# One activation table at a time in the recurrent branch: copies, grouped gelus, and the softplus ahead of its loop

## The chip, the cores and the metric

The kernel runs on one core of a Trainium2 chip. The metric is the device time of one execution in microseconds (us). The engines are named as in the profile: PE (TensorE, matmuls) with PEld (its weight loads), DVE (VectorE), ACT (ScalarE), POOL (GpSimd) and SP (SyncE, whose queue issues nearly all DMAs).

## The reference

One layer of a hybrid network on 512 tokens of width 1024, with 16 meta tokens in front (528 positions). One large projection gives the inputs of two branches, a recurrent one and a retention one; a convolutional feed-forward layer follows. What the change touches is the recurrent branch:

```python
z = xn @ w_in[l]
u_rnn, u_gate, q, k, v, g_ret, ga, gb = jnp.split(z, IN_SPLITS, axis=-1)
xr = causal_dwconv(u_rnn, rnn_conv_w[l], rnn_conv_b[l])        # 4 taps, 1280 channels
hr = rg_lru(xr, ...)
o_a = hr * jax.nn.gelu(u_gate)

def rg_lru(x, w_a, b_a, w_x, b_x, lam):                        # 10 blocks of 128 channels
    r = sigmoid(x @ w_a + b_a);  i = sigmoid(x @ w_x + b_x)    # block by block
    log_a = -8 * r * softplus(-lam)
    a = exp(log_a)
    b = sqrt(-expm1(2 * log_a)) * (i * x)
    # h[t] = a[t] * h[t-1] + b[t]
```

## The kernel before

Channels lie on the 128 partitions and positions along the free axis. Every float32 matrix is held as a float16 high part and a float16 low part, and a product is three matmuls (high x high, high x low, low x high: `SPLIT`). A `split` is one ACT instruction (the high part, line 94) and one DVE instruction (the low part, line 95). Weights come in units of up to 1 MB through three staging buffers `raw`. A unit of 8 x 256 rows and columns becomes two tiles `wt`; it serves two channel blocks. The splits of the units to come are queued as steps. `tick()` issues the next step if no more than `ahead` tiles are split in advance, and `get(u)` issues all that unit u still needs.

The recurrent branch works on 10 blocks of 128 channels (`NR`), n = 0 to 9, in two loops.

The convolution loop (line 689) takes for each n the projection of block n (`conv_product`; blocks 0 to 2 had half of it earlier), the two gate products of block n - 3 (`rnn_gates`, with two sigmoids on ACT and one product on DVE), the four taps of block n (`conv_taps`: an identity on ACT, three multiply-adds on DVE, which free the PSUM buffer), and the split of the convolved block (`conv_split`). For n < 6 the projection runs with `turns`: for each of the eight slices of the depth it does both halves of the positions with the high weights and the high input, then both with the high weights and the low input, then both with the low weights. Block n uses the weights of unit n // 2. At n = 2 a `tick()` issues the split of the first tile of unit 2, at n = 3 that of the second, both of which block 4 is the first to use.

Behind this loop stand the 23 small DVE instructions and the two of ACT that compute the softplus of lambda for all channels (lines 711 to 727), and then the gate loop (line 732). For each n it projects block n of u_gate and takes the gelu straight out of PSUM (line 737). For n < 3 it also does the gates of blocks 7, 8 and 9. A table `SPREAD` places the rest, five blocks at a time: tangents `rnn_tanh` (n = 2 and 4), exponentials `rnn_decay` with two DVE products each (n = 3 and 5), roots `rnn_root` (n = 7 and 9), and the first five scans `rnn_scan` (a DVE product and a DVE scan, n = 7).

Up to line 754 the order of PE, ACT and DVE is written out by hand (`manual_schedule`): each of these engines issues its instructions in the order of the program. Instructions that stand behind it may be slipped in between by the planner, and from there on the planner orders the work by its own costs and by program order as the priority. What follows is the rotary stage: for each of four heads `rotary` projects the queries and then the keys (two PSUM buffers each), DVE multiplies each by the cosine and the sine (`t`, lines 773 to 775), which frees the buffers, and ACT and DVE split the result (`qk`). `between(i)` is called behind each of these eight steps: for i < 5 it does scan 5 + i, and it multiplies the finished blocks with their gelus and splits them (`branch_a`, `oa`). There are four PSUM buffers (`acc`) from n = 2 of the convolution loop on, used in turn by all of these products.

Each function of ACT belongs to a table that must be loaded; the instruction that loads it shows in the profile as ACT_TABLE_LOAD on the line of the function that needs it.

Of the kernel before, what the change touches and what calls it, by code (L numbers as in the profile page):

```python
# [8 lines left out]
F32 = mybir.dt.float32  # L9
F16 = mybir.dt.float16  # L10
AF = mybir.ActivationFunctionType
ORDERED = {mybir.EngineType.PE, mybir.EngineType.Activation, mybir.EngineType.DVE}
ALU = mybir.AluOpType

P = 128
# [6 lines left out]
NR = DR // P  # L22
# [4 lines left out]
TQ = T - T0  # L27
# [5 lines left out]
SW = 2.0 ** 8  # L33
S_XN = 4.0
# [19 lines left out]
def hybrid_block_kernel(ctx, tc, x, meta, norm_mix_g, w_in, conv_w, conv_b, rg_a_w, rg_a_b,  # L54
                        rg_x_w, rg_x_b, lam, w_brnn, w_bret, w_out, norm_ffn_g, w_up,
                        fconv_w, fconv_b, w_down, norm_final_g, rope_t, decay_t, out):
    nc = tc.nc
    const = ctx.enter_context(tc.tile_pool(name="const", bufs=1))
# [17 lines left out]
    def acc(name):  # L76
        return psum["acc"].tile([P, 2, 512], F32, name=name, tag="acc")
# [9 lines left out]
    def piece(shape, dtype, name):  # L87
        return pieces.tile(shape, dtype, name=name, tag="s")

    def wtile(name):  # L90
        return work.tile([P, T], F32, name=name, tag="w")
# [101 lines left out]
    def unit_load(cuts=1):  # L193

        nk, ncol, parts, fast = units[len(loaded)]
        raw = wraw.tile([P, 2048], F32, name="raw")
        n = nk * ncol
        rv = raw[:, :n].rearrange("p (k c) -> p k c", k=nk)
        for k0, c0, ap in parts:
            load(rv[:, k0:k0 + ap.shape[1], c0:c0 + ap.shape[2]], ap)  # L200
        loaded.append(len(loaded))
        if fast:
            return fast_steps(rv, nk // 2, ncol // 2)
        hk = nk // 2
        hn = hk * ncol
        tiles = []

        def step(i, c):
            def run():
                if c == 0:  # L210
                    tiles.append(wsp.tile([P, 2, 1024], F16, name="wt"))
                sl = slice(c * hn // cuts, (c + 1) * hn // cuts)
                split(tiles[i][:, 0, sl], tiles[i][:, 1, sl], raw[:, i * hn:(i + 1) * hn][:, sl], SW)
            return run

        wviews.append(lambda a, k, c0, m: tiles[k // hk][:, a, k % hk * ncol + c0:k % hk * ncol + c0 + m])
        return [step(i, c) for i in range(2) for c in range(cuts)]
# [74 lines left out]
    ahead = [6]  # L292
    current = [0]

    def unit_tiles(u):
        return 4 if units[u][3] else 2

    def emit_step():
        u, run = steps[done[0]]
        while len(loaded) < min(u + 3, len(units)):  # L300
            queue(unit_load())
        run()
        done[0] += 1

    def queue(new):
        steps.extend((len(loaded) - 1, run) for run in new)
# [9 lines left out]
    def tick(n=1, late=True):  # L316


        for _ in range(n):
            if done[0] == len(steps):  # L320
                if len(loaded) == len(units):
                    return
                queue(unit_load())
            u = steps[done[0]][0]
            if sum(unit_tiles(i) for i in range(current[0], u + 1)) > ahead[0]:
                return
            if gating[0] and not late and hasattr(steps[done[0]][1], "late"):
                return
            emit_step()
# [10 lines left out]
    vt1 = const.tile([P, P], F32, name="vt1")  # L340
# [72 lines left out]
    def x_of(hi, lo):  # L413
        tv = (hi, lo)
        return lambda a, k, c0, n: tv[a][:, k, c0:c0 + n]
# [7 lines left out]
    def run_of(ps, halves, j=0, n=None):  # L423
        c0 = 512 - halves[0][1] + j
        n = n or halves[0][1] + halves[1][1]
        return ps.rearrange("p a b -> p (a b)")[:, c0:c0 + n]

    def project(ps, w, col, src, halves, nk, turns=False):

        both = [0, 1]  # L430
        for hfs in [both] if turns else [[0], [1]]:
            for k, (aw, ax), hf in [(k, s, hf) for k in range(nk) for s in SPLIT for hf in hfs]:
                    c0, n = halves[hf]
                    nc.tensor.matmul(half_of(ps, halves, hf), w(aw, k, col, P), src(ax, k, c0, n),  # L434
                                     start=k == 0 and (aw, ax) == (0, 0), stop=k == nk - 1 and aw == 1)
# [6 lines left out]
    HQ = [(XF + T0, 256), (XF + T0 + 256, 258)]  # L442
# [167 lines left out]
    half_r, half_t, half_x, gate_g = {}, {}, {}, {}  # L610

    def part(hv, n):
        if n not in hv:
            hv[n] = piece([P, T], F32, "rnn")
        return hv[n]
# [27 lines left out]
    def conv_taps(n, ps):  # L643
        xv = part(half_x, n)
        nc.scalar.activation(xv, run_of(ps, HR, 3, T), AF.Identity, scale=cwr[:, 30 + n:31 + n], bias=b_conv[:, n:n + 1])
        for j in (2, 1, 0):
            nc.vector.scalar_tensor_tensor(xv, run_of(ps, HR, j, T), cwr[:, 10 * j + n:10 * j + n + 1], xv,
                                           op0=ALU.mult, op1=ALU.add)
# [6 lines left out]
    def rnn_gates(n):  # L655
        xs = xr_split.pop(n)
        xr = part(half_x, n)
        gi = wtile("gi")
        for nm, bias, dst in (("a", b_a, part(half_r, n)), ("x", b_x, gi)):
            ps = acc("ps")  # L660
            wt = gw[nm][0][n // 4]
            project(ps, lambda a, k, c0, m: wt[:, a, n % 4 * P:n % 4 * P + P], 0, x_of(xs[:, 0], xs[:, 1]), HG, 1)
            nc.scalar.activation(dst, run_of(ps, HG), AF.Sigmoid,
                                 scale=1.0 / (SW * S_XR), bias=bias[:, n:n + 1])
        nc.vector.tensor_mul(xr, xr, gi)

    def rnn_tanh(n):
        nc.scalar.activation(part(half_t, n), part(half_r, n), AF.Tanh, scale=cpos[:, n:n + 1])
# [11 lines left out]
    def rnn_scan(n):  # L680
        r, t, xr = part(half_r, n), part(half_t, n), part(half_x, n)
        nc.vector.tensor_mul(t, t, xr)
        nc.vector.tensor_tensor_scan(xr, r, t, 0.0, op0=ALU.mult, op1=ALU.add)

    LAG = 3
    load_gates("a")
    load_gates("x")
    queue(unit_load())
    for n in range(NR):
        ps = conv_product(n)  # L690
        if n == 0:
            split_gates("a")
        if n >= LAG:
            tick(2 if n in (4, 6, 8) else 1)
            rnn_gates(n - LAG)
        conv_taps(n, ps)
        if n == 0:
            conv_split(0)
        if n == 1:
            split_gates("x")  # L700
        if n == 2:
            tick()
            conv_split(1)
            psum_layout(acc=4)
        if n >= 2:
            conv_split(n)


    lv = vt1[:, 70:80]
    sp = const.tile([P, 8, NR], F32, name="sp")  # L710
    nc.vector.tensor_scalar(sp[:, 0], lv, -1.0, 0.0, op0=ALU.mult, op1=ALU.max)
    nc.scalar.activation(sp[:, 1], lv, AF.Abs)
    nc.scalar.activation(sp[:, 2], sp[:, 1], AF.Exp, scale=-1.0)
    nc.vector.tensor_scalar_add(sp[:, 3], sp[:, 2], 2.0)
    nc.vector.reciprocal(sp[:, 4], sp[:, 3])
    nc.vector.tensor_mul(sp[:, 4], sp[:, 4], sp[:, 2])
    nc.vector.tensor_mul(sp[:, 5], sp[:, 4], sp[:, 4])
    nc.vector.memset(sp[:, 6], 1.0 / 15.0)
    for m in (13, 11, 9, 7, 5, 3, 1):
        nc.vector.tensor_mul(sp[:, 6], sp[:, 6], sp[:, 5])  # L720
        nc.vector.tensor_scalar_add(sp[:, 6], sp[:, 6], 1.0 / m)
    nc.vector.tensor_mul(sp[:, 6], sp[:, 6], sp[:, 4])
    nc.vector.scalar_tensor_tensor(sp[:, 7], sp[:, 6], 2.0, sp[:, 0], op0=ALU.mult, op1=ALU.add)
    cneg = const.tile([P, NR], F32, name="cneg")
    cpos = const.tile([P, NR], F32, name="cpos")
    nc.vector.tensor_scalar_mul(cneg, sp[:, 7], -8.0)
    nc.vector.tensor_scalar_mul(cpos, sp[:, 7], 8.0)


    ahead[0] = 6  # L730
    SPREAD = ((rnn_tanh, 2, 0), (rnn_decay, 3, 0), (rnn_tanh, 4, 5), (rnn_decay, 5, 5), (rnn_root, 7, 0), (rnn_scan, 7, 0), (rnn_root, 9, 5))
    for n in range(NR):
        ps = acc("ps")
        u, col = u_ug[n // 2], (n % 2) * P
        project(ps, get(u), col, xf, HQ, KD)
        tick()
        nc.scalar.activation(part(gate_g, n)[:, :TQ], run_of(ps, HQ),
                             AF.Gelu_apprx_tanh, scale=1.0 / (SW * S_XN))
        if n < LAG:
            rnn_gates(NR - LAG + n)  # L740
        for f, n0, m0 in SPREAD:
            if n == n0:
                for i in range(m0, m0 + 5):
                    f(i)

    oa = {}

# [30 lines left out]
            split(dst[m][:, 0, :n], dst[m][:, 1, :n], turned[m][:, :n], s)  # L778

    def between(i):  # L780
        if i < 5:
            rnn_scan(5 + i)
        for n in ((i,), (5, 6), (7, 8), (9,))[max(0, i - 4)]:
            branch_a(n)

# [442 lines left out]
    for i in range(2):  # L1228
# [5 lines left out]
        ps = branch(u_ba, oa_of, NR)  # L1234
# [311 lines left out]
    for j in range(12):  # L1546
# [21 lines left out]
        else:  # L1568
# [4 lines left out]
            for m in range(2):  # L1573
                f = 2 * j + m
# [210 lines left out]
```

## Time and profile before

| | us |
|---|---|
| median of 3 runs | 1058.48 (1058.31 to 1058.50) |
| the profiled execution | 1058.55, span 1056.8 |
| PE busy | 1038.8 (98%) |
| DVE busy | 872.0 (83%) |
| ACT busy | 594.3 (56%) |
| mean granted clock of PE | 0.999 |

The span runs from the first to the last instruction. A row of the timeline has the start, the length, the engine, the line, the operation, output<-input, the shape and the count; in brackets stands the idle time of the engine before it and what ended it. Rows of the groups have the count, then busy time and the mean in ns, then idle time. Matmuls are pipelined, so neighbouring rows of PE overlap.

### The profile page before, as it was taken

The page shows a single profiled execution, that of the slowest core. Times are in us where ns is not written, and L with a number is a line of the kernel's source. Part 1 is how long each engine was busy: PE and PEld are TensorE (multiplying, and loading weights), DVE is VectorE, ACT ScalarE, POOL GpSimd, SP SyncE. Part 2 cuts the span into 40 slices and gives each one's busy share as a digit, 9 for nine tenths or more (in the row PEclk, how much of TensorE's full clock was granted, in tenths as well). Part 3 has the DMA queues.
Part 4 walks back from the last instruction along what each step waited for, and adds up shares of the span by engine and source line. Part 5 has one row for each costly group of instructions (what it writes and reads, how often), then busy time and mean ns, then how long its engine had stood idle before and what let it go on. Part 6 is the DMA issues. An engine that isn't in the chain of part 4 may idle for free.

```text
span 1056.8 us, 21446 instructions
## 1 busy us (share of the span) xinstructions
PE 1038.8 (98%) x9187; PEld 866.2 (82%) x9187; DVE 872.0 (83%) x1327; ACT 594.3 (56%) x942; POOL 6.9 (1%) x20
## 2 busy tenths in 40 slices
PE   8999999999999999999999999999999999999997
PEld 6888888875588888888888886588888888888884
DVE  6885799989669999997797785479989898988965
ACT  7558973444356758666454453375555555454432
POOL 2000000000000000000000000000000000000000
PEclk9999999999999999999999999999999999999999
DMA  9241253331013132334333355032433324114312
GB/s 295 94 132 58 81 180 120 123 120 41 1 41 113 49 106 74 102 111 154 102 115 120 111 209 180 1 120 81 160 102 99 120 81 144 58 61 145 96 41 80
DMA packets 109311, 111.52 MB, mean 106 GB/s; under 512 B 5674, under 2 KB 101136, under 8 KB 109216
## 3 DMA queue, kind: packets, MB, share of 16 engines
q1 hardware_dynamic: 108640, 109.74, 32.5%
q8 instruction: 72, 1.18, 0.5%
q10 hardware_dynamic: 288, 0.27, 0.1%
q0 software_dynamic: 288, 0.14, 0.1%
q14 instruction: 23, 0.19, 0.1%
HBM read 108.04 MB, written 2.10 MB: 104 GB/s over the span
## 4 chain that ended last, share of the span: by engine, by line
PE 74%; DVE 15%; ACT 8%; issue 2%; DMA 0%; ACTq 0%; DVEq 0%
PE ps L434 27%; PE P L1603 10%; PE pa L886 9%; DVE wt L95 4%; PE pe L886 4%; PE ps L1320 4%; PE pm L434 3%; PE ps L448 3%; PE pb L886 2%; PE ps L950 2%; PE pa L1490 2%; ACT wt L94 2%; PE ps L1040 2%; PE pa L974 1%; DVE raw L262 1%
## 5 line engine op out<-in xcount | busy, mean ns | idle before, releaser
L434 PEld LDWEIGHTS <-wt 128*128 128x128 f16 x3840 | 372.8, 97 | 53.4 <-issue 1.3
L95 DVE SCALAR_TENSOR_TENSOR wt<-raw,wt 128x1024 f16<-128x1024 f32 (+2 forms) x286 | 310.4, 1102 | 54.0 <-ACT wt L94 52.9
L94 ACT ACTIVATE wt<-raw 128x1024 f16<-128x1024 f32 (+2 forms) x286 | 267.8, 958 | 117.8 <-PE P L1603 23.1
L886 PEld LDWEIGHTS <-wt 128*128 128x128 f16 x2016 | 195.3, 97 | 32.4 <-issue 5.7
L434 PE MATMUL ps<-x2h,wt 128*128 128x258 f16 (+1 forms) x1184 | 196.2, 273 | 0.0
L434 PE MATMUL ps<-xh,wt 128*128 128x258 f16 (+4 forms) x1056 | 177.5, 275 | 1.6 <-DVE t L773 1.6
L434 PE MATMUL ps<-x2l,wt 128*128 128x256 f16 (+1 forms) x592 | 161.0, 272 | 0.0
L434 PE MATMUL ps<-xl,wt 128*128 128x256 f16 (+4 forms) x528 | 140.8, 274 | 0.0
L1603 PE MATMUL P<-wt,act 128*128 128x256 f16 x792 | 88.3, 273 | 0.0
L1603 PEld LDWEIGHTS <-act 128*128 128x128 f16 x792 | 77.4, 98 | 9.0
L886 PE MATMUL pa<-xs,wt 128*128 128x258 f16 x576 | 71.3, 273 | 1.9 <-ACT kept L892 1.5
L1468 DVE SCALAR_TENSOR_TENSOR cv<-ps,vt,cv 128x512 f32<-128x512 f32 x80 | 59.5, 747 | 9.1 <-ACT cv L1466 8.5
L434 PE MATMUL pm<-oa,wt 128*128 128x256 f16 (+1 forms) x480 | 54.1, 273 | 0.0
L262 DVE TENSOR_TENSOR raw<-raw 128x1024 f32<-128x1024 f32 x43 | 52.5, 1220 | 0.7
L886 PE MATMUL pa<-ob,wt 128*128 128x257 f16 x384 | 45.7, 274 | 0.6 <-ACT last L892 0.5
L1320 PE MATMUL ps<-wt,mx 128*128 128x512 f16 x192 | 44.3, 379 | 0.0
L950 PE MATMUL ps<-wt,xh 128*128 128x512 f16 x128 | 38.3, 379 | 0.7 <-ACT qk L94 0.5
L1466 ACT ACTIVATE cv<-ps,vt,vt 128x512 f32<-128x512 f32 x40 | 30.5, 766 | 11.9 <-PE ps L434 11.9
L1490 PEld LDWEIGHTS <-wt 128*128 128x128 f16 x336 | 32.6, 97 | 4.4
L1320 PEld LDWEIGHTS <-mx 128*128 128x128 f16 x192 | 17.6, 98 | 18.5
L94 ACT ACTIVATE qk<-t 128x514 f16<-128x514 f32 (+1 forms) x16 | 10.2, 638 | 39.6 <-DVE t L775 39.6
L448 PEld LDWEIGHTS <-wt 128*128 128x128 f16 x288 | 27.9, 97 | 5.0 <-issue 0.5
(327 smaller groups left out, 1504.5 us busy)
## 6 DMA issues: line engine op xcount, KB each, us to landing
raw<-in_w_in SPq DMA_DIRECT2D x36, 1024.0 KB, 5.1
raw<-in_w_up SPq DMA_DIRECT2D x24, 1024.0 KB, 5.2
raw<-in_w_down SPq DMA_DIRECT2D x48, 256.0 KB, 3.7
raw<-in_w_branch_ret SPq DMA_DIRECT2D x16, 512.0 KB, 4.9
raw<-in_w_in SPq DMA_DIRECT2D x12, 512.0 KB, 4.8
raw<-in_w_branch_rnn SPq DMA_DIRECT2D x8, 640.0 KB, 4.7
raw<-in_w_out SPq DMA_DIRECT2D x4, 1024.0 KB, 5.1
xin<-in_x SPq DMA_DIRECT2D x4, 512.0 KB, 5.8
```

What stands on the lines that cost most here:

```text
L94: a = nc.scalar.activation(hi, src, AF.Copy, scale=s)
L95: b = nc.vector.scalar_tensor_tensor(lo, src, s, hi, op0=ALU.mult, op1=ALU.subtract)
L262: nc.vector.tensor_tensor(pair, pair, rv[:, :, right].rearrange("p (h k) c -> p h k c", h=2), op=ALU.add)
L434: nc.tensor.matmul(half_of(ps, halves, hf), w(aw, k, col, P), src(ax, k, c0, n), start=k == 0 and (aw, ax) == (0, 0), stop=k == nk - 1 and ...
L448: mm = nc.tensor.matmul(half_of(ps, halves, hf), w(aw, k, col, P), src(ax, k, c0, n), start=k == 0 and (aw, ax) == (0, 0), stop=k == KD - ...
L886: nc.tensor.matmul(ps[:, :n], ws[k // 4](wf, aw, k % 4), src(xf_, ax, k), start=first and k == 0 and (aw, ax) == (0, 0), stop=k == last_k ...
L950: nc.tensor.matmul(pb, xf(ax, k, XF + j0, nb), w(aw, k % 4, 0, 512), start=i == 0, stop=i == 23)
L1320: nc.tensor.matmul(ps[:, n], mx[k][:, a, c0:c0 + P], wo[k // 2](aw, k % 2, n * 512, 512), start=k == 0 and (a, aw) == (0, 0), stop=k == ks ...
L1466: nc.scalar.activation(vv_, taps[2], AF.Identity, scale=vt2[:, 96 + ch:97 + ch], bias=bias)
L1468: nc.vector.scalar_tensor_tensor(vv_, taps[j], vt2[:, 48 * j + ch:48 * j + ch + 1], vv_, op0=ALU.mult, op1=ALU.add)
L1490: nc.tensor.matmul(ps[:, :258], w(wf, aw, k), x2_form(xf_, ax, k), start=first and k == 0 and (aw, ax) == (0, 0), stop=k == 3 and aw == 1, ...
L1603: nc.tensor.matmul(pd[:, 256 * tt:256 * tt + 256], t[:, ax, c0 + tt * P:c0 + tt * P + P], w(wf, aw, i), start=q % 6 == 0 and tt == 0 and i ...
```

## The change

The softplus becomes a function that is called at n = 2 of the convolution loop, ahead of that turn's `tick()`; its series is written with fewer instructions (16 on DVE). The tangent of block n - 3 is taken in turn n of that loop, those of blocks 7, 8 and 9 in the gate loop. In the gate loop the projections of blocks 0 to 4, 6 and 7 leave PSUM as plain copies; the gelus of 0 to 4 are taken together at n = 5, those of 6 and 7 at n = 8, and blocks 5, 8 and 9 have theirs straight out of PSUM. The exponentials stand at n = 2, 3 and 4, the roots at n = 6 and 7, scans 0 to 7 at n = 7, 8 and 9. The gates of block 7 stay at n = 0, those of 8 and 9 are both at n = 1. `between` keeps scans 8 and 9.

```diff
+    def softplus():
+        lv = vt1[:, 70:80]
+        sp = const.tile([P, 8, NR], F32, name="sp")
+        nc.vector.tensor_scalar(sp[:, 0], lv, -1.0, 0.0, op0=ALU.mult, op1=ALU.max)
+        nc.scalar.activation(sp[:, 1], lv, AF.Abs)
+        nc.scalar.activation(sp[:, 2], sp[:, 1], AF.Exp, scale=-1.0)
+        nc.vector.tensor_scalar_add(sp[:, 3], sp[:, 2], 2.0)
+        nc.vector.reciprocal(sp[:, 4], sp[:, 3])
+        nc.vector.tensor_mul(sp[:, 4], sp[:, 4], sp[:, 2])
+        nc.vector.tensor_mul(sp[:, 5], sp[:, 4], sp[:, 4])
+        nc.vector.tensor_scalar_mul(sp[:, 6], sp[:, 5], 1.0 / 15.0)
+        for m in (13, 11, 9, 7, 5, 3):
+            nc.vector.scalar_tensor_tensor(sp[:, 6], sp[:, 6], 1.0 / m, sp[:, 5], op0=ALU.add, op1=ALU.mult)
+        nc.vector.scalar_tensor_tensor(sp[:, 6], sp[:, 6], 1.0, sp[:, 4], op0=ALU.add, op1=ALU.mult)
+        nc.vector.scalar_tensor_tensor(sp[:, 7], sp[:, 6], 2.0, sp[:, 0], op0=ALU.mult, op1=ALU.add)
+        nc.vector.tensor_scalar_mul(cneg, sp[:, 7], -8.0)
+        nc.vector.tensor_scalar_mul(cpos, sp[:, 7], 8.0)
@@ the convolution loop
             rnn_gates(n - LAG)
         conv_taps(n, ps)
+        if n >= LAG:
+            rnn_tanh(n - LAG)
...
         if n == 2:
+            softplus()
             tick()
             conv_split(1)
             psum_layout(acc=4)
@@ the gate loop; the softplus that stood ahead of it is gone
-    SPREAD = ((rnn_tanh, 2, 0), (rnn_decay, 3, 0), (rnn_tanh, 4, 5), (rnn_decay, 5, 5), (rnn_root, 7, 0), (rnn_scan, 7, 0), (rnn_root, 9, 5))
+    FIRST = {1: (rnn_tanh, (7,)), 2: (rnn_tanh, (8, 9)), 5: ("gelu", range(5)), 6: (rnn_root, range(5)), 7: (rnn_root, range(5, 10)),
+             8: ("gelu", (6, 7))}
+    THEN = {2: (rnn_decay, (0, 1)), 3: (rnn_decay, range(2, 6)), 4: (rnn_decay, range(6, 10)),
+            7: (rnn_scan, range(3)), 8: (rnn_scan, (3, 4)), 9: (rnn_scan, range(5, 8))}
+
+    def gate_gelu(i, src=None, s=1.0):
+        g = part(gate_g, i)[:, :TQ]
+        nc.scalar.activation(g, g if src is None else src, AF.Gelu_apprx_tanh, scale=s)
+
     for n in range(NR):
         ps = acc("ps")
         u, col = u_ug[n // 2], (n % 2) * P
         project(ps, get(u), col, xf, HQ, KD)
         tick()
-        nc.scalar.activation(part(gate_g, n)[:, :TQ], run_of(ps, HQ),
-                             AF.Gelu_apprx_tanh, scale=1.0 / (SW * S_XN))
-        if n < LAG:
-            rnn_gates(NR - LAG + n)
-        for f, n0, m0 in SPREAD:
-            if n == n0:
-                for i in range(m0, m0 + 5):
-                    f(i)
+        for what in (FIRST, THEN):
+            f, ms = what.get(n, (None, ()))
+            for m in ms:
+                (gate_gelu if f == "gelu" else f)(m)
+        if n in (5, 8, 9):
+            gate_gelu(n, run_of(ps, HQ), 1.0 / (SW * S_XN))
+        else:
+            nc.scalar.activation(part(gate_g, n)[:, :TQ], run_of(ps, HQ), AF.Copy, scale=1.0 / (SW * S_XN))
+        for i in ((7,), (8, 9))[n] if n < 2 else ():
+            rnn_gates(i)
@@ between
-        if i < 5:
-            rnn_scan(5 + i)
+        if i < 2:
+            rnn_scan(8 + i)
```

More of the change, by code (lines that the diff above doesn't have):

```diff
@@ L683, in rnn_scan @@
         nc.vector.tensor_tensor_scan(xr, r, t, 0.0, op0=ALU.mult, op1=ALU.add)
+    cneg = const.tile([P, NR], F32, name="cneg")
+    cpos = const.tile([P, NR], F32, name="cpos")
+    def softplus():
[15 more added lines that the diff above has]
+        nc.vector.tensor_scalar_mul(cpos, sp[:, 7], 8.0)
     LAG = 3
@@ L706, in hybrid_block_kernel @@
             conv_split(n)
[L709 to L727, printed above, removed]
-    ahead[0] = 6
-    SPREAD = ((rnn_tanh, 2, 0), (rnn_decay, 3, 0), (rnn_tanh, 4, 5), (rnn_decay, 5, 5), (rnn_root, 7, 0), (rnn_scan, 7, 0), (rnn_root, 9, 5))
+    ahead[0] = 6
+    FIRST = {1: (rnn_tanh, (7,)), 2: (rnn_tanh, (8, 9)), 5: ("gelu", range(5)), 6: (rnn_root, range(5)), 7: (rnn_root, range(5, 10)),
[5 more added lines that the diff above has]
+        nc.scalar.activation(g, g if src is None else src, AF.Gelu_apprx_tanh, scale=s)
     for n in range(NR):
```

## The prediction

> **What bounds the kernel now.** The first two rows of the page are read first.
>
> ```profile
> span 1056.8 us, 21446 instructions
> PE 1038.8 (98%) x9187; PEld 866.2 (82%) x9187; DVE 872.0 (83%) x1327; ACT 594.3 (56%) x942; POOL 6.9 (1%) x20
> ```
>
> TensorE (PE) works 1038.8 of 1056.8 us, so 18.0 us are all that can be won without taking matmuls away, and this change takes none away. The next view is the table of stretches around the change: the convolution loop (30 to 82), the gate loop (82 to 137.9), and the rotary stage in two parts. Its columns are length, then busy time of PE, PEld, DVE (VectorE), ACT (ScalarE), POOL, then granted clock and DMA.
>
> ```profile
> 30.00:82.00 52.00, 52.00 (x458) 44.30 (x456) 42.92 (x57) 31.86 (x46) 0.00 (x0) 1.00 0.34 112
> 82.00:137.90 55.90, 55.90 (x510) 49.22 (x508) 37.38 (x67) 53.04 (x68) 0.00 (x0) 1.00 0.25 81
> 147.00:184.00 37.00, 35.40 (x316) 30.25 (x315) 37.00 (x50) 12.02 (x15) 0.00 (x0) 1.00 0.52 171
> 184.00:240.00 56.00, 55.55 (x458) 43.71 (x456) 53.02 (x84) 23.20 (x36) 0.00 (x0) 1.00 0.35 115
> ```
>
> The reader is to see that PE has no idle time at all in the two loops that are edited (52.00 of 52.00, 55.90 of 55.90). ACT is nearly full in the gate loop (53.04 of 55.90), but nobody on PE waits for it. PE loses its first time one stage later, 1.6 us of 37, and there DVE is full (37.00 of 37). The waits of PE and the timeline say on what:
>
> ```profile
> PE ps L434 <- DVE t L773: 1.6, 2, 1.0
> PE ps L950 <- ACT qk L94: 0.5, 1, 0.5
> ```
>
> ```profile
> 182.67 0.27 PE L434 MATMUL ps<-xh,wt 128*128 128x256 f16 x1 [1.00 <-DVE t L773]
> ```
>
> So the stage is priced like this: time freed on ACT is worth nothing by itself; time freed on DVE before 184 us is worth at most 1.6 us (2.1 with the third wait); and any time by which an edit makes PE wait in the two loops is paid in full.
>
> **The change, part 1: the table loads.** The groups of ACT from 86 to 147 us:
>
> ```profile
> L737 ACT ACT_TABLE_LOAD x7 | 9.0, 1283 | 0.1
> L668 ACT ACTIVATE rnn<-rnn,cpos 128x528 f32<-128x528 f32 x10 | 6.5, 724 | 0.0
> L737 ACT ACTIVATE rnn<-ps 128x514 f32<-128x514 f32 x10 | 6.0, 596 | 0.1
> L663 ACT ACT_TABLE_LOAD x3 | 3.8, 1283 | 0.1
> L672 ACT ACT_TABLE_LOAD x2 | 2.6, 1283 | 0.0
> L678 ACT ACT_TABLE_LOAD x2 | 2.6, 1283 | 0.0
> L713 ACT ACT_TABLE_LOAD x1 | 1.3, 1283 | 0.0
> ```
>
> These are 15 loads. The new order needs four in the gate loop (exponential at n=2, gelu at n=5, root at n=6, gelu at n=8). That is 11 fewer, 11 x 1.283 = 14.1 us. Seven gelus (0 to 4, 6, 7) become a copy out of PSUM and a second pass: 7 x 0.596 = 4.2 us more. Seven tangents leave for the convolution loop: 7 x 0.724 = 5.1 us less. ACT therefore has about 53.0 - 14.1 + 4.2 - 5.1 = 38 us of work in 55.9 us. On PE this is worth 0, since PE does not wait for ACT there; the copies free their PSUM buffers as promptly as the gelus did. The moved tangents lie in a gap that ACT has in every turn of the convolution loop while it waits for the taps (the 2.76 us in the row of ACT below; there the tangent's 0.72 us fits): 0.
>
> One load is new further on: the gate loop now ends with gelu's table, so the root of the first head (L1057) loads its own.
>
> ```profile
> 294.33 0.39 ACT L892 ACTIVATE kept<-pa 128x257 f32<-128x257 f32 x1 [0.32 <-PE pa L886]
> 296.04 0.69 ACT L1057 ACTIVATE rt<-ps,eps_t 128x514 f32<-128x514 f32 x1 [1.32 <-PE ps L1055]
> ```
>
> ACT idles 1.32 us before that root and a load takes 1.283: hidden, 0. If it were not, 1.3 us would fall on ACT, and the root and DVE's work behind it would be 1.3 us later; PE waits for neither there now.
>
> **Part 2: the softplus moves to n=2 of the convolution loop.** This is the step to look at, because the order on DVE and ACT in this region is that of the program, and on DVE sixteen small instructions now stand between the taps of n=2 and the weight split of `tick()`. DVE there now:
>
> ```profile
> 36.77 2.37 DVE L647 SCALAR_TENSOR_TENSOR rnn<-ps,cwr,rnn 128x528 f32<-128x528 f32 x3
> 39.06 1.22 DVE L95 SCALAR_TENSOR_TENSOR wt<-raw,wt 128x1024 f16<-128x1024 f32 x1
> 40.19 1.32 DVE L95 SCALAR_TENSOR_TENSOR xs<-rnn,xs 128x528 f16<-128x528 f32 x2
> 41.43 1.22 DVE L95 SCALAR_TENSOR_TENSOR wt<-raw,wt 128x1024 f16<-128x1024 f32 x1
> 43.40 0.71 DVE L665 TENSOR_TENSOR rnn<-rnn,gi 128x528 f32<-128x528 f32 x1 [0.75 <-ACT gi L663]
> 44.09 2.37 DVE L647 SCALAR_TENSOR_TENSOR rnn<-ps,cwr,rnn 128x528 f32<-128x528 f32 x3
> ```
>
> The softplus as it stands now, after the loop:
>
> ```profile
> 87.36 0.17 DVE L714 TENSOR_SCALAR sp<-sp 128x10 f32<-128x10 f32 x1 [0.83 <-ACT sp L713]
> 87.56 0.22 DVE L715 RECIPROCAL sp<-sp 128x10 f32<-128x10 f32 x1
> ...
> 91.33 0.17 DVE L723 SCALAR_TENSOR_TENSOR sp<-sp 128x10 f32<-128x10 f32 x1
> ...
> 91.61 0.17 DVE L727 TENSOR_SCALAR cpos<-sp 128x10 f32<-128x10 f32 x1
> 91.69 1.22 DVE L95 SCALAR_TENSOR_TENSOR wt<-raw,wt 128x1024 f16<-128x1024 f32 x1
> ```
>
> Each step that uses the one before it takes about 0.206 us from start to start (87.56 to 91.33 holds 18 starts), those that do not about 0.08. The new chain has sixteen: three independent ones at 0.08, thirteen dependent ones at 0.206 with 0.05 more for the reciprocal: 0.24 + 2.68 + 0.05 = 3.0 us. Its exponential is in time: on ACT the absolute value (0.2), a load (1.28) and the exponential (0.21) come behind the identity of n=2 and end at about 36.5, before DVE is through with the taps at 39.1, and ACT has room for them:
>
> ```profile
> 34.83 1.05 ACT L94 ACTIVATE wt<-raw 128x1024 f16<-128x1024 f32 x1
> 39.18 0.64 ACT L94 ACTIVATE xs<-rnn 128x528 f16<-128x528 f32 x1 [2.76 <-DVE rnn L647]
> ```
>
> What is queued behind the sixteen is the split at 39.06, which writes the low parts of the first tile of unit 2. Who waits for it: unit 2 holds the weights of channel block 4 (`u_ur[4]`), and its projection is the next one on PE. It runs with `turns`, so the low parts are the weights of its fifth matmul:
>
> ```profile
> 39.96 0.39 PE L434 MATMUL ps<-xh,wt 128*128 128x266 f16 x2
> 40.19 0.39 PE L434 MATMUL ps<-xl,wt 128*128 128x266 f16 x2
> 40.42 0.62 PE L434 MATMUL ps<-xh,wt 128*128 128x266 f16 x4
> ```
>
> ```profile
> 45.49 1.51 PE L434 MATMUL ps<-xs,gw 128*128 128x264 f16 x12
> 46.84 0.39 PE L434 MATMUL ps<-xh,wt 128*128 128x266 f16 x2
> ```
>
> The split ends at 39.06 + 1.22 = 40.28 and is used at 40.42: a margin of 0.1 us. Put 3.0 us later it ends at about 43.3, so PE stands still for 3.0 - 0.1 = 2.9 us in the middle of a projection. The next candidates are then covered. The second tile's low parts come at 45.6 and are used at about 46.1. The projection of block 5 (46.84 now, 49.7 then) waits for the PSUM buffer of block 3, whose taps (44.09 + 2.37) end at 48.6 then, 0.75 us of DVE's idle having absorbed part of the delay. With the first stall gone, this buffer would stall PE by 1.8 us in its place. Bounds: below, 0 if the split were not held up (a gain is excluded, as a later operand speeds nothing up); above, 16 x 0.206 = 3.3 with no margin. I take 2.9, by the rows of the same sixteen kinds of instruction.
>
> After the loop ACT loses its 1.7 us and DVE its 4.3 us of softplus: off PE's path, 0.
>
> **Part 3: scans earlier, DVE relieved in the rotary stage.** Roots 0 to 9 are done by n=7 instead of n=9, and scans 0 to 7 stand in the gate loop; only 8 and 9 remain in `between`, which had 5 to 9. The groups of DVE from 137.9 to 184 us:
>
> ```profile
> L683 DVE TENSOR_TENSOR_SCAN rnn<-rnn 128x528 f32<-128x528 f32 x8 | 10.0, 1253 | 0.0
> L682 DVE TENSOR_TENSOR rnn<-rnn 128x528 f32<-128x528 f32 x7 | 4.8, 697 | 0.0
> ```
>
> Three scans with their products, 3 x (1.25 + 0.70) = 5.9 us, leave a stretch in which DVE is full, and PE's two waits there sum to 1.6. DVE can take them: in the gate loop it works 37.38 of 55.90. The rotary products (`t`) that release the PSUM buffers are then not late. I take -1.6. Bounds: -2.1 if the 0.5 at L950 goes as well; +1.0, one such wait more, if the planner, which orders what stands behind the hand-ordered region by its own costs, puts other work ahead of them. The wait at L950 belongs to the last head's keys, long after the last scan: I leave it.
>
> The gates 7 to 9 move one turn earlier. Their matmuls are the same; they use four PSUM buffers in a row, and the copy of turn 1 frees the one that the ninth needs 1 us ahead: 0. No DMA is added; the splits that free the staging buffers, and so SP's loads, keep their places in the program.
>
> **The sum.** +2.9 - 1.6 = +1.3 us. The profiled execution took 1058.55 us, 1.75 above its span and 0.07 above the median of 1058.48. So the sum is 1059.85 for it and 1059.8 for the median.
>
> **A rule weighed against the rows.** Through the idle of PE that the trace does have (up to 1.0 us in the rows above) the granted clock stays 1.00. The Trainium skill, page "TensorE: Matmul & The Clock Gate", section "Why this matters for your kernels", says that idle gaps above about 3 us between bursts bring the clock down to half, and its Part 1 gives one idle window of about 3.4 us as the condition. By that rule a stall of 2.9 us is just short of it, and the sum stays; if it were a little longer, an estimate from that page (3.4 us at half speed) adds 1.7, 1061.5. No row of this trace shows a gap that long. Because the stall is so near, I keep the drop as a rival.
>
> **The rivals.**
> *The rotary waits stay (slower).* The mechanism: behind the hand-ordered region DVE's work is set by the planner, and if it fills the freed time with the products of `branch_a` or splits just ahead of the `t` rows, the buffers are late again. Place: 168 to 184 us. Price: the -1.6 is lost, +2.9, 1061.4 us. It decides for "slower" as soon as less than 0.8 of the 1.6 is won. For it: in both places now a scan stands ahead of the late rows. Against: with 5.9 us less work DVE should have slack.
> *The stall does not come.* If the split were issued before the sixteen, only -1.6 would remain: 1056.9 us. For it: nothing but PE's clean 52.00 now; against it: after the loop the split at 91.69 now stands behind the softplus in just this way.
> *The clock drops.* A halved clock for the 44 matmuls left of that projection (0.115 us each, 40.42 to 45.49) costs up to 5.0 more: 1064.8 us.
> *ACT paces the gate loop after all.* Nine loads fewer over the whole kernel (-11, +1 at n=2, +1 at the root) less the second passes: -11.5 + 4.2 = -7.3, 1051.1 us. Against it stands PE's 55.90 of 55.90. The Trainium skill, page "ScalarE: Activation LUTs", section "Table sets: the hidden batching unit", says to batch activations by table set; the rows agree that a load costs 1.283 us, and that PE does not feel it.
>
> **How the numbers follow.** Forecast (stall, rotary waits gone) 0.58, own range 1058.9 to 1060.6; rotary waits stay 0.18; no stall 0.14; clock drops 0.05; ACT paces 0.05. The 0.2% that can be told from no change is 2.1 us, so the line runs from 1056.4 to 1060.6. Faster: ACT's case 0.05 and the edge of "no stall" if the third wait goes too, 0.05: 0.10. Slower: rotary waits 0.18, clock 0.05, the upper edge of the forecast 0.03: 0.26. Same: 0.64. The range reaches from the case without the stall, 1056.9 less the 0.5 of the third wait, to the rotary case with the larger bound of the stall: 1056.4 to 1061.8; it leaves out only the last two cases.
>
> **What would show it.** Right: a wait of PE near 40.4 us of about 2.9, put down to DVE's `wt` split; sixteen `sp` rows on DVE from 39.1; no PE wait on `t` between 160 and 190; four table loads in the gate loop and ACT idle there; one load before the first L1057. Wrong: no PE idle between 30 and 85; waits on `t` still there; or a granted clock below 1.00 after 40 us.

## The result and the profile after

| | us |
|---|---|
| before, 15 executions | 1058.48 median (1058.31 to 1058.92) |
| after, 15 executions | 1061.01 median (1059.25 to 1061.22) |
| ratio | 1.0021, 95% interval 1.0013 to 1.0029 |
| the profiled execution of after | 1059.40, span 1057.6, granted clock 0.999 |

The changed kernel is slower by about 0.2%, with the whole interval above 1. Its times fall in two groups that matter below: 12 of the 15 lie at 1060.73 to 1061.22 us with a mean granted clock of 0.996 to 0.998, three at 1059.25 to 1059.56 us with 0.999, and the profiled execution is one of the three. (A single execution of several of these kernels, before among them, is also some 2 us longer for another reason, as is the profiled one of `long` below, whose matmul of L553 near the start comes at 14.47 us instead of 12.34.)

The page's first rows, and the waits of PE from 30 to 300 us:

```profile
span 1057.6 us, 21436 instructions
PE 1038.7 (98%) x9187; PEld 866.2 (82%) x9187; DVE 870.9 (82%) x1319; ACT 587.1 (56%) x940; POOL 6.9 (1%) x20
```

```profile
PE ps L434 <- DVE wt L95: 2.7, 1, 2.7
PE ps L963 <- ACT qk L94: 0.5, 1, 0.5
```

ACT lost 7.2 us of work (594.3 to 587.1), DVE 1.1, PE nothing. The two waits on the rotary products (1.6 us) are gone; one of 2.7 us on a weight split is new. The table of stretches, the rotary stage at 150 to 187 because PE arrives there later:

```profile
30.00:82.00 52.00, 49.32 (x433) 41.70 (x431) 44.74 (x72) 35.83 (x52) 0.00 (x0) 1.00 0.33 108
82.00:140.80 58.80, 58.80 (x536) 51.75 (x534) 41.72 (x52) 48.27 (x69) 0.00 (x0) 1.00 0.23 74
150.00:187.00 37.00, 37.00 (x333) 32.12 (x332) 36.91 (x51) 13.64 (x18) 0.00 (x0) 1.00 0.51 168
```

The convolution loop, full before, has 2.68 us without PE; the rotary stage, 1.6 short before, is full. The stall on PE, and DVE's rows at the same place:

```profile
40.02 0.39 PE L434 MATMUL ps<-xl,wt 128*128 128x266 f16 x2
43.09 0.64 PE L434 MATMUL ps<-xh,wt 128*128 128x266 f16 x4 [2.68 <-DVE wt L95]
```

```profile
36.61 2.37 DVE L647 SCALAR_TENSOR_TENSOR rnn<-ps,cwr,rnn 128x528 f32<-128x528 f32 x3
38.89 0.16 DVE L691 TENSOR_SCALAR sp<-vt 128x10 f32<-128x10 f32 x1
...
41.74 0.17 DVE L704 TENSOR_SCALAR cpos<-sp 128x10 f32<-128x10 f32 x1
41.82 1.22 DVE L95 SCALAR_TENSOR_TENSOR wt<-raw,wt 128x1024 f16<-128x1024 f32 x1
```

The softplus holds DVE from 38.89 to 41.82, 2.93 us; the split behind it ends at 43.04, and the fifth matmul, which needs it, starts at 43.09. Between the profiled executions the account closes: +2.68 for the stall, -1.6 for the rotary waits, and one wait among the first 30 us 0.2 shorter (1.0 instead of 1.2) make +0.88; the two times differ by 0.85. The other 1.7 us, in 12 of 15 executions, are not in this trace.

### The profile page after: what moved, and what is told of

It reads as the page before. It is cut to its first block, busy times and chain, and to the rows that moved or that the text cites. A ratio compares the mean times of both kernels' runs of the same rounds, so it can differ in the third digit from the quotient of the medians.

```text
span 1057.6 us, 21436 instructions
## 1 busy us (share of the span) xinstructions
PE 1038.7 (98%) x9187; PEld 866.2 (82%) x9187; DVE 870.9 (82%) x1319; ACT 587.1 (56%) x940; POOL 6.9 (1%) x20
## 4 chain that ended last, share of the span: by engine, by line
PE 82%; DVE 12%; ACT 4%; issue 2%; DMA 0%; DVEq 0%; ACTq 0%
PE ps L434 35%; PE P L1616 10%; PE pa L899 9%; PE pe L899 4%; PE ps L1333 4%; DVE wt L95 3%; PE pm L434 3%; PE pb L899 2%; PE ps L963 2%; PE pa L1503 2%; PE ps L1053 2%; PE ps L448 2%; PE pa L987 1%; ACT wt L94 1%; DVE raw L262 1%
## 5 line engine op out<-in xcount | busy, mean ns | idle before, releaser
L1053 PE MATMUL ps<-sc,v 128*128 128x257 f16 (+4 forms) x384 | 31.7, 236 | 0.0
```

Source lines behind the costliest of these rows:

```text
L1053: nc.tensor.matmul(ps[:, hf, s0 - lo_i:257], vd, st[SCP[b][0]][:, sa, o:o + hi_i - s0], start=i == 0, stop=i == len(todo) - 1)
```

## Experiments

Each comparison below ran both kernels on one chip; before had a median of 1058.70, 1058.68 and 1058.66 us in the three sessions (`again`, `warm`, `only_softplus`, `back`; then `spread`, `t_first`, `swap`, `short`; then `spread_late`, `spread_tan`, `reload`, `long`).

### What the stall costs

**again** is the changed kernel, unedited, for a trace of the longer group.

> The changed kernel once more, unchanged, for a trace of its longer executions. Its times came in two groups, near 1059.4 us (granted clock 0.999) and near 1061.0 (0.996 to 0.998). Theory (clock): PE's 2.7 us of idle at 40 us makes the clock drop for one stretch in most executions; a trace of the long group then shows a granted clock below 1.00 for 3 to 4 us right behind that idle, and matmuls at twice their pitch there, worth 1.7 us. Rival (a second wait): the clock stays, and the long group has another wait of 1.7 us somewhere that the short one has not.

Median 1061.29 us, ratio 1.0016 (1.0008 to 1.0025): five of 11 executions at 1059.35 to 1059.69 with the clock at 0.999, six at 1061.29 to 1061.46 with 0.996 to 0.998. The profiled one is of the longer group (1061.46, span 1059.6). Its waits are those of the trace above. Its stretches behind the stall differ in the granted clock, the third number from the end:

```profile
43.00:45.00 2.00, 1.56 (x10) 1.14 (x11) 2.00 (x4) 1.85 (x3) 0.00 (x0) 0.74 0.00 0
45.00:47.00 2.00, 2.00 (x11) 1.36 (x10) 2.00 (x3) 0.00 (x0) 0.00 (x0) 0.50 0.05 8
47.00:49.00 2.00, 2.00 (x17) 1.64 (x16) 1.59 (x3) 0.30 (x1) 0.00 (x0) 0.91 0.94 323
```

and its matmuls beside the same ones of the trace above:

```profile
43.44 0.64 PE L434 MATMUL ps<-xh,wt 128*128 128x266 f16 x4 [2.68 <-DVE wt L95]
44.31 1.09 PE L434 MATMUL ps<-xh,wt 128*128 128x266 f16 x4
```

```profile
43.80 0.62 PE L434 MATMUL ps<-xh,wt 128*128 128x266 f16 x4
```

The shares of half clock are 2 x 0.26 / 0.5 = 1.0, then 2.0, then 2 x 0.09 / 0.5 = 0.4: 3.4 us at half speed, which is 1.7 us lost, right behind the stall. The two spans differ by 2.0, of which 0.35 is a later start (43.44 against 43.09).

**warm** keeps PE busy through the stall: 13 matmuls of 512 columns, of no use, ahead of block 4's projection.

```diff
+            for _ in range(13 if n == 4 else 0):
+                nc.tensor.matmul(ps[:, 0], w(0, 0, col, P), xf(0, 0, 0, 512), start=True, stop=True)
```

> The changed kernel with 13 matmuls of 512 columns more on PE ahead of block 4's projection (about 2.8 us of PE, written over by the projection), so that PE works while the split is late. Theory (clock): the delay stays, the idle goes, and with it the drop: all executions near 1059.5, clock 0.999. Rival (second wait): two groups as before, 1059.5 and 1061.1.

1059.65 us (1059.52 to 1059.99, one group), ratio 1.0008 (0.9999 to 1.0017). PE has no wait between 30 and 190 us and the clock stays whole where it fell before:

```profile
45.00:47.00 2.00, 2.00 (x19) 1.68 (x18) 2.00 (x3) 0.00 (x0) 0.00 (x0) 1.00 0.03 4
```

With useless work in the gap the same delay is 1.6 us cheaper. It is the idleness that halves the clock, not the lateness.

**only_softplus** is the kernel before with the softplus alone moved to n = 2 in its new form.

> The kernel before with nothing changed but the softplus, moved to n=2 in its new form. Theory: the same wait of 2.7 us on the split at 40 us and the same two groups of times, 1.7 us apart; as PE comes 2.7 us later to the rotary stage and ACT does not, part of the 1.6 us of waits there goes: 1059.6 to 1061.2 in the short group, 1061.3 to 1062.9 in the long one. Rival: the wait belongs to the tangents in the convolution loop, and without them it is under 1 us: 1058.5 to 1059.5.

1062.40 us (1062.34 to 1062.52, six executions, all with the clock at 0.997), ratio 1.0034 (1.0021 to 1.0046). Waits of PE:

```profile
PE ps L434 <- DVE wt L95: 2.7, 1, 2.7
PE ps L434 <- DVE t L774: 1.0, 1, 1.0
```

The stall needs nothing else of the change. One rotary wait of 1.0 stays of the 1.6. The sum 1058.70 + 2.7 - 0.6 + 1.7 = 1062.5 is within 0.1 of what was measured. The two groups that were expected did not come: all six executions are of the longer one.

**short** leaves the six series terms of the softplus out (its decay is that of a shorter sum), **long** adds eight multiplications by 1 to it, each as long as one of its other steps.

```diff
-        for m in (13, 11, 9, 7, 5, 3):
+        for m in ():
```

> The changed kernel without the six terms of the softplus series (six DVE instructions, 1.19 us; it leaves out terms of the sum, so its decay is another). The wait near 41 us shrinks from 2.68 to about 1.5 us. Theory A (the clock is halved behind an idle stretch only where enough of it falls in one stretch of the throttle's own): with 1.5 us idle none or few executions are halved: one group of times near 1058.4 + 1.5 - 0.5 = 1059.4 at most, clock 0.999. Theory B (any idle of over 1 us does it): groups 1.7 us apart as in the changed kernel, most executions near 1060.

```diff
+        for m in range(8):
+            nc.vector.tensor_scalar_mul(sp[:, 6], sp[:, 6], 1.0)
```

> The changed kernel with eight more small DVE instructions (0.2 us each) in the softplus: the wait near 41 us grows from 2.68 to about 4.3 us. Theory A (the longer the idle stretch, the more executions have half the clock behind it): all executions are halved: one group near 1056.7 + 4.3 + 1.8 = 1062.8, clock 0.996 to 0.997, none near 1061.0. Theory B (the share of halved executions has nothing to do with the length beyond 2.7 us): two groups again, 1061.0 and 1062.8, about one in four in the short one.

`short`: 1058.37 us, ratio 1.0000 (0.9991 to 1.0009), stall 1.45. Nine of 11 executions lie at 1058.25 to 1058.60; the other two, at 1060.3, have clocks of 0.998 and 0.999, which is no drop that the mean shows, so that nearly all or all of them kept the clock: theory A. `long`: 1063.28 us (1063.22 to 1065.47, five executions), ratio 1.0048 (1.0035 to 1.0060), none near the 1061.0 that it would take without the drop: theory A again, with a price 0.5 higher than written. Its profile says why (this execution began 2.1 us late):

```profile
46.88 1.07 PE L434 MATMUL ps<-xh,wt 128*128 128x266 f16 x4 [4.33 <-DVE wt L95]
```

```profile
45.00:47.00 2.00, 0.12 (x1) 0.13 (x2) 1.90 (x7) 1.64 (x3) 0.00 (x0) 0.50 0.00 0
47.00:49.00 2.00, 2.00 (x10) 1.35 (x10) 2.00 (x3) 0.00 (x0) 0.00 (x0) 0.50 0.00 0
49.00:52.00 3.00, 3.00 (x17) 2.04 (x15) 2.93 (x5) 0.00 (x0) 0.00 (x0) 0.54 0.52 164
```

Half clock lasts 2.0 + 2.0 + 3 x 0.46 / 0.5 = 6.8 us here, twice 3.4; its first 1.9 us pass while PE still waits, so 4.9 are felt, 2.4 us.

**swap** puts both weight splits and the splits of `xs` ahead of the softplus.

```diff
-            softplus()
-            tick()
+            tick(2)
             conv_split(1)
...
             conv_split(n)
+        if n == 2:
+            softplus()
```

(In turn 3 the `tick` that would issue the second split is left out.)

> The changed kernel with the two weight splits of turn n=2 and the splits of xs recorded ahead of the softplus, and no weight split recorded in turn 3. Prediction's claim: the wait on the weight split goes, and block 5's PSUM buffer, which waits for the taps of block 3 that now stand behind the softplus on DVE, stalls PE by some 1.8 us in its place, with DVE rnn named as what ended it: 1058.4 + 1.8 = 1060.2 us without a drop of the clock after it, 1061.9 with one. Rival (there is slack for the whole softplus once no split waits behind it): no wait between 30 and 85 us and 1058.4.

1058.53 us, ratio 1.0000 (0.9991 to 1.0009). The wait on the split is gone and one on block 3's taps stands in its place, as the prediction said that it would:

```profile
48.51 0.40 PE L434 MATMUL ps<-xh,wt 128*128 128x266 f16 x2 [1.54 <-DVE rnn L647]
```

It is 1.54 us against 1.8 expected; ten of 11 executions lie within 1058.33 to 1058.76. The 1060.2 written before the run left out the 1.6 us of rotary waits that the changed kernel saves; with them it is 1058.6, so this gap costs about its length and no slow clock.

### Where the rotary waits went

**back** is the changed kernel with the softplus behind the convolution loop again and all ten tangents in turn 2 of the gate loop.

```diff
-        if n >= LAG:
-            rnn_tanh(n - LAG)
...
-            softplus()
...
+    softplus()
...
-    FIRST = {1: (rnn_tanh, (7,)), 2: (rnn_tanh, (8, 9)), 5: ...
+    FIRST = {2: (rnn_tanh, range(10)), 5: ...
```

> The changed kernel with the softplus put back behind the convolution loop and all ten tangents in the gate loop at n=2; copies, grouped gelus, exponentials, roots and scans as in the change. Theory: the stall at 40 us (2.7) is gone, with it the drop of the clock, and the 1.6 us of the rotary waits stay won: 1058.5 - 1.6 = 1056.9, all executions in one group, no PE idle between 30 and 190 us. Rival (the stall moves): the PSUM buffer of another block is late in place of the split and 1 to 2 us stay, 1058 to 1059.

1058.44 us, ratio 0.9994 (0.9985 to 1.0002). The 1056.9 that was expected was missed: no stall stands in the loops, but two rotary waits do:

```profile
PE ps L434 <- DVE t L784: 1.3, 2, 0.8
```

```profile
156.85 2.50 DVE L761 TENSOR_TENSOR rnn<-rnn 128x514 f32<-128x514 f32 x4
159.27 0.69 DVE L785 TENSOR_TENSOR t<-ps,rope 128x514 f32<-128x514 f32 x1
```

Four products of `branch_a` stand ahead of the rotary products that free PE's buffers, the very mechanism of the first rival. Two readings were then open: that these waits are hidden in the changed kernel only because PE comes 2.7 us late, or that something else in `back` is late.

**spread** decides: the softplus is cut up (its ACT part at n = 2, its DVE part in five pieces at n = 3 to 7), tangents 0 to 5 are taken at n = 8 and 9 and the rest in turns 1 and 2 of the gate loop.

```diff
+        if 3 <= n <= 7:
+            next(softplus_dve)
+        for i in {8: range(3), 9: range(3, 6)}.get(n, ()):
+            rnn_tanh(i)
```

> The changed kernel, but with the softplus cut up: its ScalarE part at n=2, its DVE part in five pieces of three or four instructions (0.4 to 0.8 us) at n=3 to 7, tangents 0 to 5 at n=8 and 9, the others in turns 1 and 2 of the gate loop. Theory: no DVE queue of 3 us stands ahead of a weight split any more, so the 2.68 us wait near 41 us goes, and with it the stretch at half clock; PE then comes to the rotary stage as early as in back, finds DVE behind there and waits some 1.3 us: 1058.4 us (1058.0 to 1058.9), granted clock 0.998 to 0.999. Rival (moving the scans ahead of the rotary stage is worth the 1.6 us, as the prediction had it): 1056.9. Rival (the pieces still push a split late): over 1059.5, with a wait on wt between 40 and 80 us.

1056.72 us (1056.55 to 1056.96), ratio 0.9982 (0.9973 to 0.9991): faster than both kernels, and no wait of PE between 30 and 190 us:

```profile
30.00:82.00 52.00, 52.00 (x458) 44.28 (x456) 45.21 (x74) 35.13 (x51) 0.00 (x0) 1.00 0.35 112
150.00:187.00 37.00, 37.00 (x334) 32.14 (x333) 36.91 (x52) 13.71 (x18) 0.00 (x0) 1.00 0.44 145
```

The expectation that PE, once on time, would find DVE behind fell; the rival's 1056.9 was right, though not its reason, as the next run shows. In `spread` the roots begin 2.6 us earlier on ACT than in `back`, and the rotary product at 159.27 in `back` comes at 157.26. Five products of `branch_a` still stand ahead of it; all of them are earlier:

```profile
154.24 3.11 DVE L775 TENSOR_TENSOR rnn<-rnn 128x514 f32<-128x514 f32 x5
157.26 0.69 DVE L799 TENSOR_TENSOR t<-ps,rope 128x514 f32<-128x514 f32 x1
```

The first load of the root's table, in `spread`, then in `back`:

```profile
118.87 1.28 ACT L678 ACT_TABLE_LOAD   x1
```

```profile
121.49 1.28 ACT L678 ACT_TABLE_LOAD   x1
```

**spread_late** puts scans 5 to 9 back between the rotary projections; **spread_tan** puts the ten tangents back in turn 2 of the gate loop; **reload** adds five one-column activations on ACT in the gate loop that bring table loads back (ten loads between 82 and 140.8 us instead of four). Each is `spread` with this one thing changed, and its cut is against `spread`.

```diff
-            7: (rnn_scan, range(3)), 8: (rnn_scan, (3, 4)), 9: (rnn_scan, range(5, 8))}
+            7: (rnn_scan, range(3)), 8: (rnn_scan, (3, 4))}
...
-        if i < 2:
-            rnn_scan(8 + i)
+        if i < 5:
+            rnn_scan(5 + i)
```

> The kernel spread, but scans 5 to 9 leave the last turn of the gate loop and stand between the rotary projections again, as scans 5 to 9 of the kernel before did in effect; everything else is as in spread. Theory A (the place of the scans in the program is what took PE's waits out of the rotary stage): PE waits on t there again, 1.0 to 1.6 us in all, and the time is 1057.7 to 1058.4. Theory B (DVE's work is the same and the planner fills it as it comes; what counts is when ScalarE delivers the roots): no wait over 0.3 us and 1056.7 to 1057.0.

```diff
-        for i in {8: range(3), 9: range(3, 6)}.get(n, ()):
-            rnn_tanh(i)
...
-    FIRST = {1: (rnn_tanh, (6, 7)), 2: (rnn_tanh, (8, 9)), ...
+    FIRST = {2: (rnn_tanh, range(10)), ...
```

> The kernel spread, but all ten tangents run in turn 2 of the gate loop, as in the kernel back; the softplus stays cut up in the convolution loop. Theory A (six tangents of 0.65 us and two more table loads make ScalarE deliver exponentials, roots, and so the scans some 2.6 us later, and DVE then comes late to the rotary products): the first scan product starts near 128.2 us as in back, not 125.6 as in spread, PE waits about 1.3 us on t between 147 and 187, and the time is 1058.0 to 1058.5. Theory B (back was held up by its softplus on DVE at 86.7 to 90.7 us, not by the tangents): no wait on t and 1056.7.

```diff
+        for f in {0: (AF.Exp,), 3: (AF.Sqrt, AF.Exp), 4: (AF.Sqrt, AF.Exp)}.get(n, ()):
+            nc.scalar.activation(again_t, eps_t, f)
```

> The kernel spread with five more one-column activations on ScalarE in turns 0, 3 and 4 of the gate loop, each of another function than its neighbours, so that about as many table loads (five to seven of 1.28 us, 6.4 to 9 us) come back as the change removed there. Theory A (ScalarE's time in the gate loop sets when the roots, the scans and so DVE's rotary products come): scans start 3 us or more later than the 125.6 us of spread, PE waits 1.3 to 4 us in the rotary stage or on its PSUM buffers, 1058.0 to 1060.7. Theory B (the prediction's part 1: table loads off ScalarE are worth nothing on PE): 1056.7 to 1057.0.

| kernel | root's first load at | PE waits on `t` | median | ratio |
|---|---|---|---|---|
| before | 130.51 | 1.6 | 1058.48 | |
| after (PE 2.68 late) | 121.36 | 0 | 1061.01 | 1.0021 |
| back | 121.49 | 1.3 | 1058.44 | 0.9994 (0.9985 to 1.0002) |
| spread | 118.87 | 0 | 1056.72 | 0.9982 (0.9973 to 0.9991) |
| spread_late | 118.74 | 0 | 1056.76 | 0.9985 (0.9976 to 0.9994) |
| spread_tan | 121.23 | 1.4 | 1058.55 | 0.9997 (0.9988 to 1.0006) |
| reload | 122.36 | 1.2 | 1058.43 | 0.9998 (0.9989 to 1.0007) |

The place of the scans changes nothing (theory B of `spread_late`): there the last one runs on DVE at 154.65 us, in `spread` at 148.48, and the rotary product comes at 157.00 and 157.26. What counts is when ACT is through: with the tangents or the table loads back on it, that product comes at 159.01 and 159.46, and the waits are back. The waits of `spread_tan` and of `reload`, and the gate loop's row of `reload` with ACT busy 57.27 of 58.80:

```profile
PE ps L434 <- DVE t L796: 1.4, 2, 0.9
```

```profile
PE ps L434 <- DVE t L802: 1.2, 1, 1.2
```

```profile
82.00:140.80 58.80, 58.80 (x535) 51.79 (x534) 40.44 (x50) 57.27 (x82) 0.00 (x0) 1.00 0.22 73
```

In the changed kernel the roots begin at 121.36, but PE is 2.68 us late as well: measured against PE it is about the time of `spread`. The lateness of PE alone does not do it: `only_softplus` keeps 1.0 of the 1.6. Nor does the wait follow the roots in proportion: from before to `back` they come 9.0 us earlier and 1.3 of the 1.6 stays; the next 2.6 us take all of it.

**t_first** leaves ACT as in `back` and changes DVE's order instead: the products of `branch_a` may be issued only behind the rotary products of their turn (`turn` is the last of these).

```diff
-            branch_a(n)
+            with tc.issue_after(turn):
+                branch_a(n)
```

> The kernel back with one thing more: the ten products of the gate with the recurrence (L761 there, 0.62 us each) may be issued only after the rotary products of the same turn. Theory A (what makes PE wait in the rotary stage is the order on DVE: four of those products and two splits stand ahead of the rotary products that free PSUM): both waits of PE on t in 147 to 187 us (0.80 and 0.54 in back) go, and the time is 1058.4 - 1.3 = 1057.1 us (1056.8 to 1057.5). Theory B (DVE has more work in that stage than time, whatever the order; it is busy 36.91 of 37 us): the waits come back later in the stage, 1.3 in all, and the time is that of back, 1058.4.

1057.03 us (1056.84 to 1057.37), ratio 0.9984 (0.9975 to 0.9993). The waits are gone although the roots come at 121.19; nothing but splits stands ahead of the product now:

```profile
154.20 2.36 DVE L95 SCALAR_TENSOR_TENSOR wt<-raw,wt 128x1024 f16<-128x1024 f32 x2
156.47 0.69 DVE L785 TENSOR_TENSOR t<-ps,rope 128x514 f32<-128x514 f32 x1
```

Either remedy is enough; the 0.3 us that `t_first` takes more than `spread` lie further on, where PE's waits on `v` and `krep` in `spread` (0.4 in all) have become two on `v` (0.7). DVE is busy 36.7 to 37.0 of 37 us in that stage in all of these kernels; that it is full is not why PE waits, but how early, and in which order, it comes to the rotary products.

## Why the prediction was right or wrong

- *The stall of part 2* was right in place, victim, cause and size. The profile's 2.68 us count from the modelled end of the matmuls before it (40.41); but rows of PE overlap, and by its neighbours' spacing (40.19 to 40.42 before) the fifth matmul would have started at 40.02 + 0.23 = 40.25. It came 2.84 us later, against 2.9. The margin was 0.1 as said: without the softplus, which took 2.93, the split would have ended at 38.89 + 1.22 = 40.11. What was said to be late next, block 5's buffer, is what `swap` shows, 1.54 against 1.8.
- *The clock* is the step that failed. It was a rival of 0.05 with up to 5.0 us to pay, and the sum stood on a clock that holds for gaps just under 3 us. By their times it dropped in 12 of 15 executions and costs 1.7. With that term the forecast's own sum would have been 1059.8 + 1.7 = 1061.5, against a median of 1061.01; without it, the three executions whose clock held, at 1059.25 to 1059.56, are within 0.6 of the 1059.8. The median lies above the forecast's own range (1058.9 to 1060.6), and above the line that the prediction drew for "same" (1060.6). It lies within the wide range, up to 1061.8, only because that was stretched to the rival whose rotary waits stay, and these went: that the number falls inside is luck. The Trainium skill's page "TensorE: Matmul & The Clock Gate" states in Part 1 that the clock falls after at least one idle window of about 3.4 us. The trace agrees with 3.4 as the length of the slow stretch (3.4 in `again`, 6.8 in `long`) and with the 1.7 that the prediction worked out from it; it disagrees on the condition, since no gap of 2.68 us holds a window of 3.4.
- *The rotary waits of part 3* went, -1.6 as said. The reason given, three scans less in that stage and so slack on DVE, was wrong: `spread_late` puts the scans back and loses nothing, and DVE is as full as before (36.91 of 37). What counts is that ACT delivers the roots earlier and DVE so comes to the rotary products in time. So the size of this term was right by luck.
- *Part 1, "time freed on ACT is worth nothing by itself"*, fell with it. PE indeed waits for nothing of ACT in the gate loop, but DVE waits there for its roots, and what DVE does later it does ahead of PE's buffers: table loads put back, with the five activations of 0.2 us that bring them, cost 1.7 us on the chip (`reload`, 1058.43 against 1056.72), the tangents 1.8. It holds for `back`, though, whose earlier roots win nothing (ratio 0.9994). The arithmetic of ACT held in all (-7.3, 7.2 measured), the four loads too. The 38 us for the gate loop did not: ACT worked 45.37 us there (82 to 137.9), since one of the loads that the sum took off lies behind 137.9 (1.3), and since five more roots, two more weight splits and two more sigmoids fall into the stretch (6.0). The load ahead of the first L1070 is hidden as said: it starts at 295.48 and PE does not wait behind it.
- *The planner's rival* (products of `branch_a` ahead of the `t` rows) did not decide here, but its mechanism is real: it is what `back` shows and `t_first` removes.

## What to carry to other kernels

Before small work is moved ahead of anything on an in-order engine, look at what is queued behind it and at its margin, and cut it into pieces that fit the gaps (`spread`: the same softplus in five pieces cost nothing). Price a stall of TensorE by its length, plus the slow clock behind it where these runs show one: 2.7 us of idle brought 1.7 us more in most executions, 1.5 us brought none that is clear. An engine that nobody waits for in its own stage may still set when another engine's backlog starts, so follow its results to the stage where a wait exists before calling its time worthless.

## What the hardware showed that was not expected

- A gap of 2.68 us on PE halved the granted clock in 24 of 32 executions, counted by their times (12 of 15, 6 of 11 and 6 of 6), for 3.4 us in the two that were profiled. Gaps of 1.45 and 1.54 us did so in at most three of 22, none of which is clear from its mean clock; a gap of 4.33 did so in five of five, in the profiled one for 6.8 us.
- Where the gap lies decides. In every trace here the changes of the clock are a whole number of 3.413 us apart (`again`: full from 6.40 us, half from 43.95, 11 x 3.413 later, full from 47.36). So the throttle looks at fixed stretches of that length, and they can be counted on from the first change (4.42 us in the changed kernel's trace above, so that one begins at 41.97). Two stretches of `again`, then the two of the trace above that share its gap:

```profile
40.54:43.95 3.41, 0.73 (x7) 0.45 (x6) 3.14 (x13) 3.38 (x5) 0.00 (x0) 1.00 0.00 0
43.95:47.36 3.41, 3.41 (x18) 2.32 (x16) 3.37 (x6) 0.90 (x2) 0.00 (x0) 0.50 0.08 17
```

```profile
38.56:41.97 3.41, 1.85 (x16) 1.20 (x13) 2.97 (x18) 2.93 (x4) 0.00 (x0) 1.00 0.00 0
41.97:45.38 3.41, 2.29 (x20) 1.96 (x21) 3.41 (x5) 2.54 (x4) 0.00 (x0) 1.00 0.00 0
```

- In `again` all 2.68 us of the gap lie in one stretch, and the next runs at half clock; in the other trace the same gap is cut into 1.56 and 1.12, and the clock stays whole. It fell behind stretches with 2.47 us idle (`only_softplus`) and 2.40 (`long`) and stayed behind 1.54 (`swap`) and 1.24 (`short`). At the end of the kernel, where the last matmul lies in the stretch, it stayed behind 1.94 (before) and fell behind 2.02 (`spread_tan`). The limit would then be near 2.0, and a gap of 2.68 would pass it in 1 - (2 x 2.0 - 2.68) / 3.41 = 0.61 of its positions, where 0.75 was counted. This is an estimate: idle time is modelled at its ends, and with so few executions 0.61 is not told from 0.75. Why all six executions of `only_softplus` dropped stays open.
